# Two accumulator pools opened in the other order, in a hybrid DeltaNet/HGRN2 block

## The chip, the cores and the metric

One core of a Trainium2 chip runs the whole block. The metric is device time in microseconds, one launch, lower is better. Each kernel is run several times, and the median is compared.

## The reference, cut to what matters

The input x is 256 tokens by 2048 channels, float32. One layer is computed:

- `n = rms_norm(h)`, then one projection of `n` gives the inputs of 16 heads, 8 of gated DeltaNet ("GDN") and 8 of HGRN2, each 128 wide.
- each head runs its own chunked recurrence, is normalised per head and multiplied by a SiLU gate.
- `h = h + concat(y_A, y_B) @ W_out`, with `W_out` 2048 by 2048. Rows 0 to 1023 of it meet the GDN heads, rows 1024 to 2047 the HGRN2 heads.
- `h = h + relu(rms_norm(h) @ W1)^2 @ W2`, hidden width 8192, and a last `rms_norm`.

## The kernel before, in words

Each large product is done with a rounded part and its remainder: for a weight tile, `split` (L114) lets ScalarE write the rounded part `hi` (L120) and VectorE the difference `lo` (L121), and TensorE adds the products into one accumulator. Three stages follow one another.

**Input projection and heads.** The loop over `n` at L738 issues the projection of head `n + 1` and then the recurrence ("mix") of head `n`. The projections accumulate in pool `psP`, tiles `acc` (`acc_p("acc")`, L331 and L332) and `tok` (L358); the latter hold the values and gates of two heads, and ScalarE copies them out at L367. The mixes accumulate in pool `psM`: small products under the tag `mx` and those of the DeltaNet solve under `sv`. Each of the two pools holds four accumulators of 128x512 float32.

An HGRN2 mix (`hgrn_mix`, L633 to L732) is one dependent chain over several engines. Gates on ScalarE and VectorE (L641 to L656), one product on GpSimd (L657), a scan on VectorE (L659), two GpSimd steps (L660, L669), decays on VectorE and an exponential on ScalarE (L665, L671, L680, L681), then TensorE: scores inside 32-wide blocks into `pd` (L695, L698) and the others into `pa` (L704 to L710). VectorE masks and sums `pd` (L713, L717), GpSimd spreads the sum into `A` (L720), ScalarE copies `pa` into `A` (L723 to L727), TensorE multiplies `A` with the values into `poh` (L729 to L731). `finish_heads` takes it on: squares and a root on ScalarE (L479 to L481), the gate on VectorE (L483), a transpose on TensorE into `pt` (L487), and `hi` and `lo` of the result into `yTa` or `yTb` (L491, L492). In the first two HGRN2 heads the steps at L657, L660, L669 and L720 (`eng`) run on VectorE instead of GpSimd; the diff leaves that as it is, and the last two heads, of which the prediction speaks, have them on GpSimd.

**Output projection** (loop at L833). For each half `nh` of the output columns, 16 steps `k`, one per head: the weight rows of head `k` are split once, and 12 matmuls of 512 columns (L847) go into four accumulators. Step `k` reads `yT(k)`, the output of head `k`, so only steps 14 and 15 read the last two HGRN2 heads, called head 6 and head 7 below. The pools of the first stage are closed before (`mctx.close()`), and two new ones of four accumulators each are opened in their place, `psA` (`acc`) and then `psB` (`accb`). Half 0 accumulates in `psA`, half 1 in `psB`.

**MLP.** Both products, in `psA` and `psB` in turn (L876 to L878).

A closed pool's place is handed to whatever is opened next, from the front: `psA` lies where the pool opened first lay, `psB` where the second one lay. A tile in a new place waits for the last use of what lay there. A scheduler then puts the instructions of each engine in an order, and each engine works its list off in that order: an instruction that waits holds up all behind it. Weight tiles of 1 MB stream in on SyncE's queue (L304, L838, L951) through three buffers, `hi` and `lo` through three each, so that the split for step `k + 3` needs the matmuls of step `k` to be done.

The few lines that fix the places are these:

```
psM = mctx.enter_context(tc.tile_pool(name="psM", bufs=MXB, space=PSUM))
psP = mctx.enter_context(tc.tile_pool(name="psP", bufs=2, space=PSUM))
...
psA = ctx.enter_context(tc.tile_pool(name="psA", bufs=4, space=PSUM))
psB = ctx.enter_context(tc.tile_pool(name="psB", bufs=4, space=PSUM))
```

Of the kernel before, what the change touches and what calls it, by code (L numbers as in the profile page):

```python
# [12 lines left out]
PSUM = bass.MemoryType.PSUM  # L13
# [62 lines left out]
def hybrid_block(ctx: ExitStack, tc: tile.TileContext, x, xt, w_in, w_ab, params, w_out, w_ff1, w_ff2,  # L76
# [19 lines left out]
    yTa = ypool.tile([P, NYA, 2 * T], F32R, tag="yT", name="yTa")  # L96
    mctx = ExitStack()
    mp = mctx.enter_context(tc.tile_pool(name="mp", bufs=1))
    psM = mctx.enter_context(tc.tile_pool(name="psM", bufs=MXB, space=PSUM))
    psP = mctx.enter_context(tc.tile_pool(name="psP", bufs=2, space=PSUM))  # L100

    def wtile():
        return wpool.tile([P, 2048], F32, tag="w", name="w")
# [1081 lines left out]
```

## Time and profile before

| | |
|---|---|
| median of 3 runs | 1251.95 us (1251.02 to 1252.16) |
| the profiled execution: its own time | 1252.03 us |
| the profiled execution: span of the trace | 1250.2 us |
| mean granted TensorE clock | 0.98 of full speed |
| busy share: TensorE, VectorE, ScalarE, GpSimd | 98%, 83%, 62%, 9% |
| chain that ended last, share on TensorE | 91% |

The span runs from the first to the last instruction; 1.8 us of the execution lie around it. PE is TensorE, DVE VectorE, ACT ScalarE, POOL GpSimd. A row of the timeline has the start, the duration, the engine, the line, and what is written and read; in brackets stand the idle time before it and what ended that. The ends of matmuls are modelled, so that matmul rows overlap; the distance from one start to the next is the measure of their rate. A 32-bit product of two unrounded operands appears as two rows per matmul.

### The profile page before, as it was taken

Reading aid. Unit: us, or ns where it says so; the run is one execution under the profiler, and the core shown is the slowest. Engines: PE = TensorE matmul, PEld = TensorE weight load, DVE = VectorE, ACT = ScalarE, POOL = GpSimd, SP = SyncE. Lnnn points to the kernel's source line nnn. Section 1 sums busy time; section 2 is a strip of 40 time slices with the busy share of each in tenths; the row PEclk is TensorE's granted clock in tenths of the full one; section 3 lists DMA queues with packets and bytes.
Section 4 is the critical chain, followed back from the end, with each engine's and each line's share of the span. In section 5 each row is a group of like instructions: output and inputs, shape, how many; then the busy total and the mean of one; then the engine's idle time right before and its main releaser. Section 6 shows DMA issues by size and latency. Waiting matters only on the chain.

```text
span 1250.2 us, 18173 instructions
## 1 busy us (share of the span) xinstructions
PE 1221.6 (98%) x6894; PEld 1017.3 (81%) x6894; DVE 1035.3 (83%) x1455; ACT 777.0 (62%) x1150; POOL 113.4 (9%) x165
## 2 busy tenths in 40 slices
PE   9999999999999959999999999999999999999997
PEld 7888888887788848888888888888888888888886
DVE  7878997797778953768888889898998888988887
ACT  7668666675668653646655655666566656656553
POOL 0132333053111110000000000000000000000000
PEclk9999999999799969999999999999999999999999
DMA  9445555543235414665465455555775555565561
GB/s 332 167 161 193 169 184 175 204 168 120 76 129 203 169 69 163 241 198 201 169 230 204 169 203 209 173 185 181 262 281 198 196 208 202 176 228 196 177 233 68
DMA packets 37144, 233.45 MB, mean 187 GB/s; under 512 B 4696, under 2 KB 5728, under 8 KB 10176
## 3 DMA queue, kind: packets, MB, share of 16 engines
q1 hardware_dynamic: 34848, 229.83, 52.4%
q0 software_dynamic: 1632, 1.72, 0.6%
q8 instruction: 54, 0.88, 0.3%
q10 hardware_dynamic: 576, 0.74, 0.2%
q14 instruction: 34, 0.28, 0.1%
HBM read 227.67 MB, written 4.60 MB: 186 GB/s over the span
## 4 chain that ended last, share of the span: by engine, by line
PE 91%; POOL 2%; DVE 2%; DMA 2%; issue 1%; ACT 1%; SPq 0%; POOLq 0%; DVEq 0%; ACTq 0%
PE acc L877 9%; PE acc L878 9%; PE acc L876 9%; PE acc L358 9%; PE accb L877 8%; PE accb L876 8%; PE accb L878 8%; PE acc L331 8%; PE acc L332 4%; PE acc L847 4%; PE accb L847 3%; PE accv L331 2%; PE accv L332 1%; POOL X L513 1%; POOL Xt L511 1%
## 5 line engine op out<-in xcount | busy, mean ns | idle before, releaser
L121 DVE TENSOR_TENSOR lo<-w,hi 128x1024 fp32r<-128x1024 f32 (+1 forms) x422 | 485.7, 1167 | 123.4 <-ACT hi L120 112.3
L120 ACT CAST hi<-w 128x1024 fp32r<-128x1024 f32 (+1 forms) x422 | 413.7, 994 | 242.5 <-PE acc L877 56.2
L331 PE MATMUL acc<-xT,hi 128*128 128x512 f32 x512 | 181.2, 400 | 0.7 <-ACT hi L120 0.7
L332 PE MATMUL acc<-xT,lo 128*128 128x256 f32 x512 | 140.9, 287 | 0.0
L120 ACT CAST hi<-TT 128x1024 fp32r<-128x1024 f32 x88 | 92.0, 1052 | 77.5 <-issue 21.7
L121 DVE TENSOR_TENSOR lo<-TT,hi 128x1024 fp32r<-128x1024 f32 x88 | 106.8, 1221 | 30.4 <-ACT hi L120 28.1
L358 PE MATMUL acc<-hi,xT 128*128 128x512 f32 x384 | 117.6, 395 | 0.0
L331 PEld LDWEIGHTS acc<-xT,hi 128*128 128x128 f32 x512 | 95.4, 190 | 20.7 <-ACT hi L120 1.2
L332 PEld LDWEIGHTS acc<-xT,lo 128*128 128x128 f32 x512 | 97.2, 191 | 5.2 <-DVE lo L121 1.9
L876 PE MATMUL acc<-hi,sets 128*128 128x512 f32 x260 | 101.4, 391 | 0.0
L877 PE MATMUL acc<-hi,sets 128*128 128x512 f32 x260 | 101.2, 390 | 0.0
L878 PE MATMUL acc<-lo,sets 128*128 128x512 f32 x260 | 95.9, 390 | 0.0
L876 PE MATMUL accb<-hi,sets 128*128 128x512 f32 x224 | 88.0, 393 | 0.0
L877 PE MATMUL accb<-hi,sets 128*128 128x512 f32 x224 | 87.3, 390 | 0.0
L358 PEld LDWEIGHTS acc<-hi,xT 128*128 128x128 f32 x384 | 71.5, 189 | 14.9
L878 PE MATMUL accb<-lo,sets 128*128 128x512 f32 x224 | 78.7, 391 | 0.0
L877 PE MATMUL acc<-hi,gs 128*128 128x512 f32 (+1 forms) x200 | 77.0, 385 | 0.0
L876 PE MATMUL acc<-hi,gs 128*128 128x512 f32 (+1 forms) x200 | 76.7, 385 | 0.0
L878 PE MATMUL acc<-lo,gs 128*128 128x512 f32 (+1 forms) x200 | 75.6, 385 | 0.0
L358 PE MATMUL acc<-lo,xT 128*128 128x512 f32 x192 | 73.5, 401 | 0.0
L877 PE MATMUL accb<-hi,gs 128*128 128x512 f32 x188 | 73.1, 389 | 0.0
L876 PE MATMUL accb<-hi,gs 128*128 128x512 f32 x188 | 72.6, 389 | 0.0
(367 smaller groups left out, 2291.5 us busy)
## 6 DMA issues: line engine op xcount, KB each, us to landing
w<-in_w_ff_dram SPq DMA_DIRECT2D x128, 1024.0 KB, 5.0
w<-in_w_in_dram SPq DMA_DIRECT2D x61, 1024.0 KB, 5.0
w<-in_w_out_dram SPq DMA_DIRECT2D x16, 1024.0 KB, 5.0
w<-in_w_in_dram SPq DMA_DIRECT2D x12, 256.0 KB, 5.7
big<-in_xt_dram SPq DMA_DIRECT2D x8, 256.0 KB, 5.8
h<-in_x_dram SPq DMA_DIRECT2D x2, 1024.0 KB, 8.8
scr_h<-h SPq DMA_DIRECT2D x4, 512.0 KB, 7.7
tail<-scr_h SPq DMA_DIRECT2D x2, 1024.0 KB, 7.0
```

What stands on the lines that cost most here:

```text
L120: ACT.copy(hi, w)
L121: eng.tensor_tensor(out=lo, in0=w, in1=hi.bitcast(F32), op=ALU.subtract)
L331: PE.matmul(accs[g], lhsT=hi[:, kk, g, :], rhs=xT[:, k, :], start=(k == 0), stop=False)
L332: PE.matmul(accs[g][:, T:], lhsT=lo[:, kk, g, :], rhs=xT[:, k, 0:T], start=False, stop=(k == KT - 1))
L358: PE.matmul(accs[hf], lhsT=xT[:, k, a + hf * P:a + hf * P + P], rhs=ww[:, cs], start=(k == 0 and a == 0 and ww is hi), stop=(k == KT - 1 a ...
L511: POOL.tensor_tensor(out=t3, in0=X[:, j, j + 1:].unsqueeze(2).to_broadcast([P, nr, ncol]), in1=X[:, j, 0:ncol].unsqueeze(1).to_broadcast([ ...
L513: POOL.tensor_tensor(out=X[:, j + 1:, 0:ncol], in0=X[:, j + 1:, 0:ncol], in1=t3, op=ALU.subtract)
L847: PE.matmul(accs[2 * hf + c], lhsT=st, rhs=ww[:, c * 512:(c + 1) * 512], start=(k == 0 and a == 0 and ww is hi), stop=(k == 2 * NH - 1 and ...
L876: PE.matmul(dst, lhsT=ah, rhs=bh, start=start, stop=False)
L877: PE.matmul(dst, lhsT=al, rhs=bh, start=False, stop=False)
L878: PE.matmul(dst, lhsT=ah, rhs=bl, start=False, stop=stop)
```

## The change

The two pools of the first stage are opened in the other order. No size, no count and no line of the computation is touched.

```
     mctx = ExitStack()
     mp = mctx.enter_context(tc.tile_pool(name="mp", bufs=1))
+    psP = mctx.enter_context(tc.tile_pool(name="psP", bufs=2, space=PSUM))
     psM = mctx.enter_context(tc.tile_pool(name="psM", bufs=MXB, space=PSUM))
-    psP = mctx.enter_context(tc.tile_pool(name="psP", bufs=2, space=PSUM))
```

So `psA` now lies where the projections' accumulators were, and `psB` where those of the mixes were. The instructions are the same ones, and up to the scores of head 6 they stand in the same order on every engine. From there on the scheduler orders them otherwise, on TensorE, VectorE and ScalarE; the lists of GpSimd and SyncE stay as they were.

On TensorE, before: the rows from the transpose of head 6 to the first matmul of the output projection.

```order
L487 MATMUL pt<-cst,ig 128x128 x2
L695 MATMUL pd<-E 32x32 x32
L698 MATMUL pd<-gx 32x64 x8
L704 MATMUL pa<-E 32x32 x4
L708 MATMUL pa<-E 64x64 x2
L710 MATMUL pa<-L 128x128
L729 MATMUL poh<-ig,A 128x128
L730 MATMUL poh<-ig,A 128x128
L731 MATMUL poh<-ig,A 128x128
L487 MATMUL pt<-cst,ig 128x128 x2
L847 MATMUL acc<-hi,yTa 128x512 x4
```

All of head 7's products stand ahead of L847 there. On TensorE, now, the end of head 6's scores:

```order
L704 MATMUL pa<-E 32x32 x4
L708 MATMUL pa<-E 64x64 x2
L710 MATMUL pa<-L 128x128
L847 MATMUL acc<-hi,yTa 128x512 x4
L847 MATMUL acc<-lo,yTa 128x512 x2
```

The output projection now follows head 6's scores directly. What is left of the two heads stands between its matmuls: `poh` of head 6 in step 3, its `pt` and head 7's `pd` in step 6, head 7's `pa` in step 8, its `poh` in step 10 and its `pt` in step 12. Step 6 shows it, on TensorE, now:

```order
L847 MATMUL acc<-hi,yTa 128x512 x8
L847 MATMUL acc<-lo,yTa 128x512 x2
L487 MATMUL pt<-cst,ig 128x128 x2
L695 MATMUL pd<-E 32x32 x32
L698 MATMUL pd<-gx 32x64 x8
L847 MATMUL acc<-lo,yTa 128x512 x2
```

A transpose that waits there holds up the matmuls of the output projection behind it. On VectorE, in head 7's chain (`uz` and the second `ig` are the gate's, `lo<-w,hi` are splits of output weights), with - for before and + for now:

```order
 L375 SCALAR_TENSOR_TENSOR uz<-ig,uz 128x512
+L121 TENSOR_TENSOR lo<-w,hi 128x1024
 L659 SCALAR_TENSOR_TENSOR gx<-cst_a,u 128x256
 L377 TENSOR_TENSOR ig<-ig,uz 128x2x256
+L121 TENSOR_TENSOR lo<-w,hi 128x1024
 L665 TENSOR_TENSOR E<-gx 128x256 x5
-L483 SCALAR_TENSOR_TENSOR ig<-poh,ss,ig 128x128 x2
+L121 TENSOR_TENSOR lo<-w,hi 128x1024
 L682 TENSOR_TENSOR gx<-gx,u 128x256
 L680 TENSOR_TENSOR E<-E,gx 128x256 x5
 L681 TENSOR_TENSOR E<-E,gx 128x512
```

The splits of steps 3, 4 and 5, which stood behind the whole chain, now stand between its links, and head 6's gate (L483) has moved back past them. ScalarE's `hi` halves of the same splits moved in the same way.

More of the change, by code (lines that the diff above doesn't have):

```diff
@@ L98, in hybrid_block @@
     mp = mctx.enter_context(tc.tile_pool(name="mp", bufs=1))
+    psP = mctx.enter_context(tc.tile_pool(name="psP", bufs=2, space=PSUM))
     psM = mctx.enter_context(tc.tile_pool(name="psM", bufs=MXB, space=PSUM))
-    psP = mctx.enter_context(tc.tile_pool(name="psP", bufs=2, space=PSUM))
     def wtile():
```

## The prediction

> **What bounds the kernel now.** I read the page first: busy shares, then the forty slices.
>
> ```profile
> span 1250.2 us, 18173 instructions
> PE 1221.6 (98%) x6894; PEld 1017.3 (81%) x6894; DVE 1035.3 (83%) x1455; ACT 777.0 (62%) x1150; POOL 113.4 (9%) x165
> ...
> PE   9999999999999959999999999999999999999997
> ...
> PEclk9999999999799969999999999999999999999999
> ```
>
> TensorE is busy 98% of the span, so it sets the time. Only one slice falls clearly out, the fifteenth (437.6 to 468.8 us): PE is at 5 tenths there, and its granted clock at 6. That is where the input projection ends and the output projection begins. The view by windows cuts this place finer. Its columns are the window, its length, busy time (and count) of PE, PEld, DVE, ACT and POOL, the granted clock, the DMA share and GB/s.
>
> ```profile
> 440.00:450.00 10.00, 5.83 (x99) 4.28 (x97) 6.61 (x13) 8.11 (x16) 1.93 (x3) 0.93 0.53 201
> 450.00:460.00 10.00, 5.17 (x101) 4.16 (x101) 8.21 (x20) 4.47 (x13) 2.21 (x3) 0.50 0.00 1
> 460.00:470.00 10.00, 5.77 (x17) 4.34 (x18) 1.33 (x4) 2.54 (x11) 0.76 (x2) 0.50 0.01 2
> ...
> 513.35:1250.20 736.85, 728.67 (x3305) 604.79 (x3303) 632.76 (x782) 444.24 (x561) 1.13 (x2) 1.00 0.56 199
> ```
>
> From 450 to 470 the clock is half, and the DMA queues are all but silent. After 513 PE is busy 728.67 of 736.85 us at full clock, and the list of waits names none of PE's in that stretch: whatever is won before 513 should reach the end. PE's timeline shows who holds PE in the gap.
>
> ```profile
> 445.35 0.49 PE L710 MATMUL pa<-L 128*128 128x128 f32 x2
> 450.25 0.76 PE L729 MATMUL poh<-ig,A 128*128 128x128 f32 x2 [4.42 <-POOL u L657]
> ...
> 454.87 0.66 PE L487 MATMUL pt<-cst,ig 128*128 128x128 f32 x2 [3.01 <-DVE ig L483]
> 456.98 1.35 PE L695 MATMUL pd<-E 128*32 128x32 f32 x64 [1.45 <-DVE E L680]
> ...
> 461.87 0.77 PE L729 MATMUL poh<-ig,A 128*128 128x128 f32 x2 [1.20 <-POOL A L720]
> ...
> 465.44 0.66 PE L487 MATMUL pt<-cst,ig 128*128 128x128 f32 x2 [1.95 <-DVE ig L483]
> 467.19 2.08 PE L847 MATMUL acc<-hi,yTa 128*128 128x512 f32 x4 [1.08 <-DVE yTb L492]
> ...
> 472.47 1.14 PE L847 MATMUL acc<-hi,yTa 128*128 128x512 f32 x4
> ...
> 475.27 1.07 PE L847 MATMUL acc<-hi,yTa 128*128 128x512 f32 x4
> ...
> 477.99 1.07 PE L847 MATMUL acc<-hi,yTa 128*128 128x512 f32 x4
> ...
> 513.35 1.98 PE L847 MATMUL accb<-hi,yTa 128*128 128x512 f32 x8
> ```
>
> Between 445.84 (445.35 + 0.49) and 467.19 PE only follows the chain of heads 6 and 7, and the first L847 starts when the chain's last link, L492, is done. Step 0 of the output projection reads head 0 of the DeltaNet group, not head 7. What it waits for is the place of its accumulator: psA lies on psM, whose last user is head 7's transpose.
>
> **The change part by part.** No instruction is added or removed. The first L847 now needs the projections' accumulators, and their last reader is a copy on ScalarE:
>
> ```profile
> 445.04 0.69 ACT L367 ACTIVATE ig<-acc,gnw 128x512 f32<-128x512 f32 x1
> ...
> 447.10 0.63 ACT L217 ACTIVATE uz<-uz 128x512 f32<-128x512 f32 x1
> ...
> 471.86 1.05 ACT L120 CAST hi<-w 128x1024 fp32r<-128x1024 f32 x1 [5.25 <-PE acc L847]
> ```
> ```profile
> 445.17 1.23 DVE L121 TENSOR_TENSOR lo<-w,hi 128x1024 fp32r<-128x1024 f32 x1 [1.44 <-ACT hi L120]
> ```
>
> It ends at 445.73, before PE is through with head 6's scores. The splits of steps 0 to 2 exist by then: the third `lo` ends at 446.40, and the fourth `hi` waits for PE to let go of the first (5.25 us of idle, ended by L847). So the output projection can start at 445.9.
>
> *Its length.* A step at full clock is 477.99 − 475.27 = 2.72 us. The first step of before took 472.47 − 467.19 = 5.28 us at half clock and the second 2.80, 2.64 us too much in all. That is lost only because PE had idled; with no gap before it, it goes. Sixteen steps are 43.52 us.
>
> *What lies between them now.* The small products of the two heads were done inside the gap at half clock, and now take room among the L847. Their price at full clock is in rows of the same lines earlier in the trace:
>
> ```profile
> 428.37 0.38 PE L729 MATMUL poh<-ig,A 128*128 128x128 f32 x2
> ...
> 428.96 0.37 PE L332 MATMUL acc<-xT,lo 128*128 128x256 f32 x1
> ...
> 438.34 0.38 PE L487 MATMUL pt<-cst,ig 128*128 128x128 f32 x2
> 438.65 0.32 PE L695 MATMUL pd<-E 128*32 128x32 f32 x12
> ...
> 441.86 0.26 PE L695 MATMUL pd<-E 128*32 128x32 f32 x6
> 442.05 0.73 PE L358 MATMUL acc<-lo,xT 128*128 128x512 f32 x2
> ...
> 443.77 0.39 PE L358 MATMUL acc<-lo,xT 128*128 128x512 f32 x1
> 444.09 0.58 PE L695 MATMUL pd<-E 128*32 128x32 f32 x44
> ```
>
> A `poh` holds the stream up for 428.96 − 428.37 = 0.59 us, a `pt` for 438.65 − 438.34 = 0.31, and all scores of a head for 0.32 + 0.26 + (445.84 − 444.09) = 2.33. Two, two and one of them are left: 1.18 + 0.62 + 2.33 = 4.13 us. They can cost no less than nothing (half 0 would end at 489.4, the time be 1228.1) and hardly more than the 8.12 us that PE was busy with them in the gap at half clock (the row by windows under the rivals; 1236.2). I take 4.13, since it comes from the same products among full-rate matmuls.
>
> *Sum.* Half 0 ends at 445.9 + 43.52 + 4.13 = 493.55, where before it ended at 513.35: 19.8 us earlier. The profiled execution's 1252.03 becomes 1232.2; the median shown lies 0.08 below that execution, less than matters here.
>
> [...]
>
> *What hides the chain now.* Steps 14 and 15 need heads 6 and 7, and PE's fixed order puts the small products at set places, so each leg of the chain has the room between two places. Before, from the rows above, against the room now (2.72 a step, the small products added):
>
> - end of head 6's `pa` to its `poh`: 450.25 − 445.84 = 4.4 us before; room to the third matmul of step 3: 454.5 − 445.84 = 8.7.
> - `poh` to `pt` of head 6: 4.6 before; room to step 6: 465.1 − 454.5 = 10.6.
> - `pd` to `poh` of head 7: 4.9 before; room to step 10: 476.7 − 465.4 = 11.3.
> - `poh` to `pt` of head 7: 3.6 before; room to step 12: 6.7.
> - `pt` to the first reader of head 7: 1.75 before; room to step 15: 7.4.
>
> Into these legs go splits. One costs ScalarE 1.05 and VectorE 1.23 us, and it may also wait for PE to release a buffer, with the chain queued behind it. The first leg: `hi` of step 3 waits for the end of step 0 at 448.6, so the exponential behind it (L656) starts near 449.7 instead of 448.36, and the rest is late by 1.3 and one `lo`, 1.23: 4.4 becomes some 7, against 8.7. The second has three splits, of steps 4 to 6, one per 2.72 us. Counted on with the same durations, head 6's gate ends near 461.8 and is wanted at 465.1. The third and fourth leave about 3 us each. So the tightest slack is some 2 to 3 us.
>
> ```profile
> 424.00 1.22 DVE L121 TENSOR_TENSOR lo<-w,hi 128x1024 fp32r<-128x1024 f32 x1 [0.84 <-ACT hi L120]
> ```
> ```profile
> 424.58 1.25 POOL L657 TENSOR_TENSOR u<-u 128x256 f32<-128x256 f32 x1 [0.80 <-ACT u L656]
> ...
> 449.51 0.72 POOL L657 TENSOR_TENSOR u<-u 128x256 f32<-128x256 f32 x1
> ```
> ```profile
> 448.36 0.63 ACT L656 ACTIVATE u<-u 128x512 f32<-128x512 f32 x1 [0.63 <-DVE u L655]
> ```
> ```profile
> w<-in_w_out_dram SPq DMA_DIRECT2D x16, 1024.0 KB, 5.0
> ```
>
> GpSimd's step takes 1.25 us beside a split on VectorE and 0.72 without one; now splits run beside all of head 7's GpSimd steps. At 0.53 us for each of five that is 2.7 us over three legs, at most 1 to 1.6 in one. Weights hold: a tile lands in 5.0 us and feeds two steps, 5.44. Half 1 needs psB, now on psM, and head 7's transpose is read some 8 us before 493.55.
>
> **The rivals.** *The chain comes late.* A slack of 2 to 3 us is small for work queued behind splits, and a late link stops PE itself, since the product that wants it stands in front of L847 rows. For it: each GpSimd row of head 7 may stretch, and VectorE has 12.6 us of chain work in this stretch. Against it: the legs' sums above. If one leg runs 3 us over its slack, the time is 1235; if two do and each stop also costs the clock, at 2.64 us, it is 1232.2 + 6 + 5.3 = 1243.5. [...]
>
> ```profile
> 445.84:467.19 21.35, 8.12 (x111) 6.26 (x111) 12.62 (x31) 9.91 (x31) 4.89 (x7) 0.57 0.09 37
> ```
>
> *Slower, by lockstep.* Were every one of the old waits paid again inside the output projection (21.35 − 8.12 = 13.2 us of idle) and the stops kept the clock at half, as from 450 to 470, all sixteen steps would cost 5.28 instead of 2.72, 41 us more. The gain of 19.8 is gone once, beside 13.2 us of stops, three more steps run cold (3 × 2.56 = 7.7). With six cold steps it is 1232.2 + 13.2 + 15.4 = 1260.8. Against it: the old waits were exposed because nothing else was queued, and now 2.72 us of ready work stands ahead of each.
>
> *No change.* The pools swap, but the wait moves to half 1, whose place is now psM: it would have to wait until 513. For that, head 7 would have to end 20 us later than the 485 worked out here. Or the placement is not what I read it to be, and the first L847 still waits for head 7; but its order, ahead of head 7's products, would then stop the program.
>
> **How the numbers follow.** The full gain, 1230.5 to 1235, has 0.80; the late chain, 1235 to 1244, 0.14; lockstep 0.03; no change 0.03. The range goes from 1230, where the small products hide better than priced, to 1241, which takes in most of the second case. Faster by over 0.2% (2.5 us, about what a measurement here can tell from no change) is 0.80 + 0.14 = 0.94, same 0.03, slower 0.03.
>
> **What would show it.** In the changed profile the fifteenth slice should read 9 for PE and for the clock, half 0 should start at 445.9 and its L847 rows come every 2.72 us from the first; `accb` should start near 493.5, and DMA should move some 190 GB/s from 450 to 470. PE's waits should name neither L483, L720 nor L492. A wait at L487 or L729 among L847 rows would show the late chain, and its length the loss; a clock of 0.50 in such a window the lockstep. If `accb` starts at 493.5 and the end does not come 19.8 us earlier, my claim that PE sets all that follows is wrong.

## The result, and the profile after

The changed kernel takes 1232.41 us, the median of 4 runs (1231.15 to 1233.91), beside 1252.06 us for the kernel before in as many (1251.02 to 1253.11). The ratio is 0.9844, with a 95% interval of 0.9826 to 0.9861. The forecast was 1232.2.

The profiled execution is the slowest of the four, 1233.91 us. Its page, busy shares first and then the slices:

```profile
span 1232.1 us, 18170 instructions
PE 1217.8 (99%) x6894; PEld 1014.9 (82%) x6894; DVE 1035.6 (84%) x1455; ACT 776.3 (63%) x1150; POOL 113.9 (9%) x165
...
PE   9999999999999999999999999999999999999997
...
PEclk9999999998799999999999999999999999999999
```

The fifteenth slice, 5 and 6 before, reads 9 for PE and for the clock. The view by windows, columns as before, puts numbers to the same place:

```profile
440.00:450.00 10.00, 10.00 (x116) 7.75 (x117) 7.68 (x14) 8.63 (x15) 0.98 (x2) 1.00 0.61 211
450.00:460.00 10.00, 10.00 (x49) 8.38 (x48) 8.84 (x17) 7.46 (x17) 3.74 (x4) 1.00 0.39 120
460.00:470.00 10.00, 10.00 (x121) 8.17 (x121) 7.90 (x13) 4.27 (x7) 0.00 (x0) 1.00 0.52 198
493.50:1232.00 738.50, 730.23 (x3310) 605.52 (x3308) 634.02 (x784) 444.64 (x561) 1.12 (x2) 1.00 0.56 199
```

PE is busy in all of every window, at full clock, and the weights keep coming. From 450 to 470 DMA moves 120 and 198 GB/s, 159 on average, where 190 was expected. PE's timeline shows what fills the stretch:

```profile
446.29 0.49 PE L710 MATMUL pa<-L 128*128 128x128 f32 x2
446.72 1.21 PE L847 MATMUL acc<-hi,yTa 128*128 128x512 f32 x4
...
449.62 1.07 PE L847 MATMUL acc<-hi,yTa 128*128 128x512 f32 x4
...
452.34 1.07 PE L847 MATMUL acc<-hi,yTa 128*128 128x512 f32 x4
...
455.51 0.38 PE L729 MATMUL poh<-ig,A 128*128 128x128 f32 x2
...
456.10 0.71 PE L847 MATMUL acc<-hi,yTa 128*128 128x512 f32 x2
...
466.19 0.38 PE L487 MATMUL pt<-cst,ig 128*128 128x128 f32 x2
466.50 0.73 PE L695 MATMUL pd<-E 128*32 128x32 f32 x62
...
467.42 0.73 PE L847 MATMUL acc<-lo,yTa 128*128 128x512 f32 x2
...
477.72 0.38 PE L729 MATMUL poh<-ig,A 128*128 128x128 f32 x2
...
484.54 0.38 PE L487 MATMUL pt<-cst,ig 128*128 128x128 f32 x2
...
491.84 1.07 PE L847 MATMUL acc<-hi,yTb 128*128 128x512 f32 x4
...
494.56 1.98 PE L847 MATMUL accb<-hi,yTa 128*128 128x512 f32 x8
```

The first L847 stands right behind L710, and no row of PE from 446 to 495 has a bracket: it waits for nothing there. Half 0 lasts 494.56 − 446.72 = 47.84 us; 47.65 was forecast, and before it was 513.35 − 467.19 = 46.16, with almost nothing between its steps. `accb` starts 18.8 us earlier than before instead of 19.8. The missing us was lost ahead of the change's place: L710 ends at 446.78 here and at 445.84 in the execution of before, and the first L847 is late by the same 0.9 (the last section shows where it was lost). From `accb` to the end of the span it takes 737.54 us against 736.85. Both differences lie within the scatter of single executions; the runs of this kernel differ by 2.8 us.

From the end of L710 to the first `accb` it was 513.35 − 445.84 = 67.51 us before, and it is 494.56 − 446.78 = 47.78 now. By the rows, the 19.7 us between them are made up of 13.2 us of idle PE, 4 us of small products (8.12 at half clock, 4.1 to 4.3 now) and some 2.5 us of cold first steps, steps at half clock.

### The profile page after: what moved, and what is told of

Read it like the earlier page. It is cut to its first block, busy times and chain, and to the rows that moved or that the text cites. A ratio compares the mean times of both kernels' runs of the same rounds, so it can differ in the third digit from the quotient of the medians.

```text
span 1232.1 us, 18170 instructions
## 1 busy us (share of the span) xinstructions
PE 1217.8 (99%) x6894; PEld 1014.9 (82%) x6894; DVE 1035.6 (84%) x1455; ACT 776.3 (63%) x1150; POOL 113.9 (9%) x165
## 4 chain that ended last, share of the span: by engine, by line
PE 91%; DMA 2%; DVE 2%; POOL 2%; issue 2%; ACT 1%; SPq 0%; POOLq 0%; DVEq 0%; ACTq 0%
PE acc L877 9%; PE acc L876 9%; PE acc L878 9%; PE acc L358 9%; PE accb L878 8%; PE accb L877 8%; PE acc L331 8%; PE accb L876 8%; PE acc L332 4%; PE acc L847 4%; PE accb L847 4%; PE accv L331 2%; PE accv L332 1%; POOL X L513 1%; POOL Xt L511 1%
```

## The experiments

The theory was the prediction's: half 0 had waited for the place of its accumulators, not for data, and ready matmuls now fill the waits of the last heads' chain. The rivals were that the exchange does something else, that a late chain costs part of the gain, and that the clock rather than the waits made the loss. The runs were made in three groups, each beside runs of the kernel before on the same chip (medians 1252.26, 1252.78 and 1252.66); the ratios of this section are to those.

**The place alone, from both sides.** The kernel before, with the output stage's pools exchanged instead of the first stage's:

```
-    psA = ctx.enter_context(tc.tile_pool(name="psA", bufs=4, space=PSUM))
     psB = ctx.enter_context(tc.tile_pool(name="psB", bufs=4, space=PSUM))
+    psA = ctx.enter_context(tc.tile_pool(name="psA", bufs=4, space=PSUM))
```

> The kernel before, its two first-stage pools in the old order (psM, then psP), but with psB opened ahead of psA, so that half 0 of the output projection accumulates where the projections did. Theory (what counts is only on whose place half 0's accumulators lie): the instructions come in the order of the changed kernel, and the time is the changed kernel's, 1232.4 us, within 2; half 0 starts near 446 to 447 us and ends near 494. Rival (the order of the pools in the first stage, or the banks the mixes and projections themselves use, made the gain): the time stays at 1252.

Measured: 1232.56 us (1232.44 to 1234.39), ratio 0.9843 [0.9828, 0.9858]. All its engines have the changed kernel's order of instructions. The windows from 450 to 470 and the start of half 1:

```profile
450.00:460.00 10.00, 10.00 (x49) 8.38 (x48) 8.89 (x16) 7.19 (x15) 4.69 (x5) 1.00 0.32 105
460.00:470.00 10.00, 10.00 (x121) 8.18 (x121) 7.99 (x14) 5.18 (x9) 0.00 (x0) 1.00 0.62 213
```
```profile
495.48 1.98 PE L847 MATMUL accb<-hi,yTa 128*128 128x512 f32 x8
```

The same edit in the changed kernel puts `psA` back on the mixes' place:

> The changed kernel (psP, then psM) with psB opened ahead of psA, so that half 0 lies on the mixes' accumulators again. Theory: the gain is gone, 1252 us within 2, with the first L847 near 467 us, after head 7's last link, and half the clock from 450 to 470. Rival (the gain comes from the projections' and mixes' own banks in the first stage): 1232.

Measured: 1252.71 us (1250.90 to 1255.33), ratio 1.0002 [0.9993, 1.0012]. The first L847 waits for L492 as before:

```profile
467.73 2.08 PE L847 MATMUL acc<-hi,yTa 128*128 128x512 f32 x4 [1.08 <-DVE yTb L492]
```

What counts is the pairing, which pool of the second stage lies on which of the first, and nothing else in the change.

**The place without the data.** The changed kernel with half 0's steps in reverse, so that it begins with head 7, and with its start and stop flags moved along:

```
-        for kp in range(8):
+        for kp in range(7, -1, -1) if nh == 0 else range(8):
...
-            for kk in range(2):
+            for kk in (1, 0) if nh == 0 else (0, 1):
...
```

> The changed kernel with half 0's sixteen steps in reverse, head 7 first; the sums are the same in another order. The place is free as in the changed kernel, but now the data of the first step is head 7's. Theory (the gain is the time in which PE has steps to do that need nothing of heads 6 and 7; the free place only allows it): the wait comes back whole, first L847 near 467 us, 1252 us within 2. Rival (the place alone, or the scheduler's other order of splits, makes the gain): 1232 to 1240.

Measured: 1252.24 us (1248.28 to 1253.56), ratio 0.9997 [0.9988, 1.0006]. The place is free, but the first step's data are not:

```profile
467.24 2.93 PE L847 MATMUL acc<-hi,yTb 128*128 128x512 f32 x6 [0.56 <-ACT yTb L491]
```

So a free place is worth nothing by itself. The gain is the work that needs neither head 6 nor head 7 and can stand ahead of them.

**Half of the place.** In the kernel before, the accumulators under `sv` and those under `mx` become two pools, and `psA` two pools of two accumulators each, so that the first two of half 0 lie on places that come free early:

```
-    psM = mctx.enter_context(tc.tile_pool(name="psM", bufs=MXB, space=PSUM))
+    psV = mctx.enter_context(tc.tile_pool(name="psV", bufs=4 - MXB, space=PSUM)); psM = mctx.enter_context(tc.tile_pool(name="psM", bufs=MXB, space=PSUM))
...
-    psA = ctx.enter_context(tc.tile_pool(name="psA", bufs=4, space=PSUM))
+    psA = [ctx.enter_context(tc.tile_pool(name=f"psA{i}", bufs=2, space=PSUM)) for i in range(2)]; nA = [0]
...
```

> The kernel before with the pools of the solve (two accumulators), the mixes (two) and the projections (four) opened in this order and psA split into two pools of two: half 0's accumulators for the first 128 tokens lie on the solve's place, free since long, those for the other 128 on the mixes'. Theory: only the first-token matmuls of the steps whose splits exist can go ahead, three buffers of them, 3 x 6 x 0.227 = 4.1 us of work, into the first wait of 4.4 us. The other waits stay, and the clock falls later by about those 4.1 us: 1246 to 1248 us. Rival (any free accumulator lets the whole stage start): 1232 to 1236. Rival (one accumulator in the mixes' place holds all back): 1252.

Measured: 1247.15 us (1246.20 to 1248.76), ratio 0.9958 [0.9943, 0.9972]. PE's timeline:

```profile
445.10 1.17 PE L847 MATMUL acc<-hi,yTa 128*128 128x512 f32 x4
...
449.61 0.46 PE L729 MATMUL poh<-ig,A 128*128 128x128 f32 x2 [0.15 <-POOL u L657]
...
454.24 0.50 PE L487 MATMUL pt<-cst,ig 128*128 128x128 f32 x2 [3.73 <-DVE ig L483]
...
466.55 2.08 PE L847 MATMUL acc<-hi,yTa 128*128 128x512 f32 x4 [1.08 <-DVE yTb L492]
```

Three half steps (445.10 to about 449.2) fill the first wait, 4.42 us before and 0.15 now. Then the ready work is used up, and the rest is paid as before. The gain, some 5 us, is about the length of the work that was moved (3 × 1.36 = 4.08 us).

In the control the first-stage pools are divided in the same way, but `psA` stays one pool of four:

> The kernel before with the solve's two accumulators, the mixes' two and the projections' four opened as three pools in this order, and psA left as one pool of four: two of half 0's accumulators lie on the solve's place and two on the mixes'. The instructions come in the order of the kernel before. Theory (a pool's first tile waits for all that lay under the pool): 1252 us within 2. Rival (a tile waits only for what lay under it): as half_place, 1246 to 1248.

Measured: 1252.11 us (1250.66 to 1253.31), ratio 0.9996 [0.9986, 1.0005].

```profile
468.05 2.08 PE L847 MATMUL acc<-hi,yTa 128*128 128x512 f32 x4 [1.08 <-DVE yTb L492]
```

Two of the four places under `psA` were free at 445, as the run before shows, and the first accumulator waited until 468 for all of them. In this program a pool's first tile waits for everything that lay under the whole pool.

**The clock by itself.** The first try at keeping the clock up in the kernel before, without moving any work, was dummy products that nobody reads, behind head 6's scores and behind its `poh`:

```
+    def dummies(a, b, n):
+        if n:
+            t = sv("dummy")
+            for _ in range(n):
+                PE.matmul(t[:, 0:b.shape[-1]], lhsT=a, rhs=b, start=True, stop=True)
...
+        dummies(xT[:, 0, 0:P], xT[:, 0, :], 18 if hd == 6 else 0)
...
+        dummies(A[:, 0:P], A[:, 0:P], 10 if hd == 6 else 0)
```

> The kernel before with 18 products of 512 columns and 10 of 128 that nobody reads (into an accumulator of the solve), put on TensorE between head 6's scores and its poh and between that poh and its transpose, so that the clock should not fall; 14 and 10 of them stand in the two longest waits, 4 a little earlier where they cost up to 0.9 us. The waits for the chain stay. Theory (of the 19.8 us, 2.64 was the cold first steps, and 8.12 - 4.13 = 4.0 the small products at half clock, most of them links of the chain): granted clock 0.9 or more from 450 to 470, and 2.64 + 4.0 - 0.9, about 4 to 6 us gained: 1246 to 1248 us. Rival (the clock is a side show, the idle time is all): 1250 to 1253. Rival (the clock is most of it): below 1240.

Measured: 1253.62 us (1252.78 to 1255.90), ratio 1.0006 [0.9997, 1.0016]. A miss: in the profiled execution, the longest of the ten, the clock fell all the same, though no wait of PE was longer than 1.95 us. Its mean clock was 0.982, that of the others 0.983 to 0.985, and 0.980 to 0.982 without the dummies. Its windows, and PE's timeline (L847 is L855 there):

```profile
450.00:460.00 10.00, 5.75 (x110) 4.77 (x108) 7.17 (x19) 4.84 (x16) 3.41 (x5) 0.86 0.00 1
460.00:470.00 10.00, 5.67 (x26) 4.35 (x27) 2.50 (x7) 2.54 (x11) 0.76 (x2) 0.50 0.01 2
```
```profile
456.07 0.50 PE L487 MATMUL pt<-cst,ig 128*128 128x128 f32 x2 [1.49 <-DVE ig L483]
458.18 1.36 PE L701 MATMUL pd<-E 128*32 128x32 f32 x64 [1.62 <-DVE E L686]
...
468.38 2.08 PE L855 MATMUL acc<-hi,yTa 128*128 128x512 f32 x4 [1.08 <-DVE yTb L492]
```

The scores behind the second of these waits already run at half speed: 1.36 us for 64 rows of L701, where 62 of the same product took 0.73 in the changed kernel.

The second try put dummies into all six waits, each group on a tile that is written no earlier than its wait begins:

```
+        dummies(ivg[:, 1, 0:P], ivg[:, 1, 0:T], 8 if hd == 6 else 0)
+        dummies(E[:, 0, 0:P], E[:, 1, :], 2 if hd == 7 else 0)
...
+        dummies(A[:, 0:P], A[:, 0:P], {6: 14, 7: 7}.get(hd, 0))
...
+        dummies(yT(NH + hd, 0, P), xT[:, 0, :], {6: 3, 7: 2}.get(hd, 0))
```

> A second try at the clock alone: the kernel before with products that nobody reads in all six waits of the gap, each group reading a tile that is written no earlier than the wait begins, so that none runs ahead of it. The waits for the chain stay, and nothing of the output projection moves. Theory (of the 19.8 us, 13.2 were idle time, 4.0 the small products at half clock, 2.6 the cold first steps): granted clock 0.95 or more from 450 to 470, small products at their full-clock prices, step 0 of the output projection 2.72 to 2.9 us; 6.6 us gained, less up to 0.9 for two groups that come in the way of the scores: 1245.5 to 1248. Rival (the clock is a side show): 1251 to 1253. If the clock falls again, the question stays open.

Measured: 1250.89 us (1249.75 to 1254.14), ratio 0.9991 [0.9980, 1.0002], which tells it neither from no change nor, surely, from a small gain. The windows of the profiled execution, again the longest of the ten, and PE's timeline (L847 is L856):

```profile
450.00:460.00 10.00, 7.56 (x61) 5.91 (x60) 7.17 (x19) 4.85 (x16) 3.41 (x5) 0.90 0.00 1
460.00:470.00 10.00, 7.51 (x105) 6.26 (x104) 2.28 (x7) 2.54 (x11) 0.76 (x2) 0.76 0.01 2
```
```profile
459.33 2.08 PE L636 MATMUL dummy<-E 128*128 128x256 f32 x4
...
465.06 0.77 PE L736 MATMUL poh<-ig,A 128*128 128x128 f32 x2 [1.93 <-POOL A L727]
...
466.48 2.59 PE L636 MATMUL dummy<-A 128*128 128x128 f32 x14
...
470.64 1.19 PE L856 MATMUL acc<-hi,yTa 128*128 128x512 f32 x4
```

The granted clock was 0.90 and 0.76 where 0.95 or more was expected: it fell twice, though it came back each time. The first step is warm here, 473.51 − 470.64 = 2.87 us by the start of the next one, so a clock that is up does spare the cold step. But the first L847 comes 3.4 us later than the 467.19 of before. Of these, 1.2 us had been lost ahead of the gap (the scores of head 6 end at 447.04 instead of 445.84); the rest is that dummies stood in the chain's way, the group on `E` amid the scores and the group on `A`. In this execution the two about cancel. Six of the ten executions took 1249.75 to 1250.90 us at a mean clock of 0.989 or 0.990, about that of the changed kernel, and the other four 1252.66 to 1254.14 at 0.985 to 0.987; only the longest has a profile. What the clock alone is worth is therefore not measured by either run.

**How much lateness the cover takes.** In the changed kernel GpSimd multiplies head 7's gate by 1.0 a number of times ahead of its scan, which makes all of head 7's chain late and changes no value:

```
         eng.tensor_tensor(out=lf[:, 0, :], in0=lf[:, 0, :], in1=lf[:, 1, :], op=ALU.add)
+        for _ in range(8 if hd == 7 else 0): POOL.tensor_scalar(lf[:, 0, :], lf[:, 0, :], 1.0, None, ALU.mult)
```

With 8, 16 and 28 passes:

> The changed kernel with eight further GpSimd passes over head 7's 128x256 log decays (times 1.0, so that nothing changes in value), 7 to 9 us more in the chain ahead of its scan. The scheduler knows of them and puts head 7's products later. Theory: the chain ended at 486 us and step 15 begins at 491.8, and the chain without its waits for PE's places is some 17 to 20 us from the scan (452.3) on, so about 20 us of delay are free: 1232.4 us within 2. Rival of the prediction, the late chain (slack of 2 to 3 us a leg is all there is): 4 to 6 us lost, 1236 to 1239.

> The changed kernel with 16 further GpSimd passes in head 7's chain; at the 1.23 to 1.27 us that one took in the kernels with 8 and 28, some 20 us more. Theory (about 20 us are covered by the sixteen steps): at the edge, 1232 to 1235 us. Rival (the cover is that of the single legs, 4 us each): 1240 or more, since 28 passes cost 14.8 us and 12 fewer would then save less than 8.

> The same with 28 further passes, 24 to 32 us more in head 7's chain. [...] If the cover is larger than worked out, 1232.

| passes | they took | time, us | ratio [interval] | PE's waits in half 0 |
|---|---|---|---|---|
| 0 (the change) | 0 | 1232.41 | 0.9844 [0.9826, 0.9861] | none |
| 8 | 9.81 us | 1231.95 (1231.73 to 1233.91) | 0.9834 [0.9819, 0.9848] | none |
| 16 | 20.04 us | 1236.59 (1235.33 to 1238.28) | 0.9874 [0.9852, 0.9895] | 1.90, 0.56 |
| 28 | 35.51 us | 1247.23 (1246.06 to 1247.73) | 0.9951 [0.9936, 0.9966] | 6.33, 1.51, 1.90, 0.56 |

The rows that carry the table: with 8 passes, on GpSimd, then with 16, on PE, and with 28, on PE (L847 is L848 in all three).

```profile
451.18 9.81 POOL L658 TENSOR_SCALAR u<-u 128x256 f32<-128x256 f32 x8
```
```profile
491.34 0.49 PE L487 MATMUL pt<-cst,ig 128*128 128x128 f32 x2 [1.90 <-DVE ig L483]
492.40 2.93 PE L848 MATMUL acc<-hi,yTb 128*128 128x512 f32 x6 [0.56 <-ACT yTb L491]
496.63 1.08 PE L848 MATMUL accb<-hi,yTa 128*128 128x512 f32 x4
```
```profile
495.12 0.44 PE L696 MATMUL pd<-E 128*32 128x32 f32 x16 [6.33 <-DVE E L681]
```

A chain that is 9.8 us late costs nothing: the scheduler puts head 7's products at later places among the L847, and the slack of the single legs does not matter. At 20.0 us the ready work runs out just before the end. The loss of some 4 us there is 1.90 + 0.56 us of waits and a last step that runs partly cold (496.63 − 492.40 = 4.23 instead of 2.72). At 35.5 us the loss is 14.8: 10.3 us of waits (6.33 + 1.51 + 1.90 + 0.56), and the rest is cold products between and behind them. The run with 16 passes came out 1.6 us above the 1235 that its expectation ended at, and the one with 28 passes 1.2 us above the 1236 to 1246 put down for it; that one's passes also took 35.5 us, longer than the 24 to 32 expected of them. Half 0 thus covers a delay of more than 9.8 and less than 20.0 us. An estimate of the point between does not hold: less its 2.5 us of waits the row with 16 passes would put it near 17.5, but the row with 28, less its 10.3, near 25.2.

## Why the prediction was right, point by point

The mechanism, the range and the path came out as forecast. That the median came within 0.2 us of 1232.2 is closer than the runs of one kernel agree (2.8 us), and in part luck, as the terms below show.

- *The wait for the place* was the cause. It is shown by the exchange from either side (0.9843 and 1.0002), and the half place shows that it can be had in parts.
- *Ready data* were the condition: with the place free and head 7 first, the gain is nil (0.9997).
- *Steps of 2.72 us.* The steps with nothing between them took 2.72 to 2.74, save the first, 449.62 − 446.72 = 2.90. The L847 of half 0 come at their full rate from its second step on.
- *Small products, 4.13 us.* The five steps with small products among them took 3.41, 4.08, 3.80, 3.42 and 2.99 us, together 4.10 more than 2.72 each. With 0.18 in the first step and 0.04 in three others, that is all of the 4.3 us (47.84 − 43.52) that the sixteen steps took over 43.52. The sum was right, its terms less so. A `poh` stands in 456.10 − 455.51 = 0.59 as priced, but the two L847 behind it take 0.1 us longer than elsewhere, so its step is 0.69 or 0.70 longer. The first `pt` and the scores made their two steps 1.36 and 1.08 longer, 2.44 where 0.31 + 2.33 was put. The 0.2 too little and the 0.2 too much cancel.
- *The change from full-width to 32-wide products and back*, in steps 6 and 8, left no cost of its own to see on top of the 4.13. But that price was itself read from 32-wide products among full-width ones, so what the change alone costs the rows do not tell. The two L847 behind the 32-wide products of step 6 took 467.99 − 467.42 = 0.57 us, against 0.46 elsewhere; behind a full-width `poh`, with no 32-wide product near, two took 456.65 − 456.10 = 0.55. From the end of L710 to `accb` the time shrank by 19.7 us, where the sum of the prediction had 19.8.
- *Slack of the legs.* It was better than the "2 to 3 us" written. The products that PE took without waiting were ready well ahead, as VectorE's rows show for the two gates and for the last link:

```profile
462.06 0.60 DVE L483 SCALAR_TENSOR_TENSOR ig<-poh,ss,ig 128x128 f32<-128x128 f32 x2
...
479.95 0.61 DVE L483 SCALAR_TENSOR_TENSOR ig<-poh,ss,ig 128x128 f32<-128x128 f32 x2 [0.58 <-ACT ss L481]
...
485.47 0.48 DVE L492 SCALAR_TENSOR_TENSOR yTb<-pt,gnw,yTb 128x256 fp32r<-128x256 f32 x1
```

Head 6's gate is done at 462.66 and its transpose is taken at 466.19, 3.5 us later. The forecast was 461.8 and 465.1, 3.3 apart; they came 0.9 and 1.1 later, with the 0.9 that the whole stage was late. Head 7's `poh` has 4.1 us (ScalarE's last copy into `A` ends at 473.62, and it is taken at 477.72), its gate 4.0 (480.56 to 484.54), the last link 5.9 (485.95 to 491.84). The tightest slack was thus 3.5 us.

- *The first leg was misread*, on the safe side. The prediction took it to lengthen from 4.4 to "some 7 against 8.7", since the list of waits puts head 6's `poh` down to L657. But `poh` reads `A` and `ig`, not `u`. What it truly waited for is ScalarE's copy into `A`, which ended at nearly the same time. PE's weight load for `poh` (PEld) tells the two apart in the kernel before:

```profile
450.22 0.50 PEld L729 LDWEIGHTS poh<-ig,A 128*128 128x128 f32 x2 [4.58 <-POOL u L657]
```

It starts at 450.22, just before L657 ends (449.51 + 0.72 = 450.23), and so it does in the two runs with divided pools (449.57 against 449.59, 451.08 against 451.09). The copy, first in the kernel before, then in the changed one, on ScalarE:

```profile
449.74 0.41 ACT L727 COPY A<-pa 32x64 f32<-32x64 f32 x2
```
```profile
450.99 0.41 ACT L727 COPY A<-pa 32x64 f32<-32x64 f32 x2
```

It ends at 450.15 there, and `poh` starts at 450.25; now it ends at 451.40 and `poh` is taken at 455.51. From the end of L710 the leg is 4.3 us before and 4.6 now. The copy stands behind the exponential (L656), which came 1.0 us later after L710, but it does not stand behind L657, and before it had waited 0.58 us for GpSimd's L720 anyway. So only 0.3 us of the lateness reached it, and the slack is 4.1 us where 8.7 − 7 = 1.7 was written.

- *GpSimd beside VectorE.* L657 stretched to 1.25 us, as priced; L669 took 1.02 instead of 0.85, and L660 its 1.13 as before. First GpSimd's rows, then VectorE's splits beside them:

```profile
451.02 1.25 POOL L657 TENSOR_TENSOR u<-u 128x256 f32<-128x256 f32 x1 [0.68 <-ACT u L656]
453.16 1.13 POOL L660 TENSOR_SCALAR gx<-gx 128x256 f32<-128x256 f32 x1 [0.89 <-DVE gx L659]
```
```profile
450.45 1.23 DVE L121 TENSOR_TENSOR lo<-w,hi 128x1024 fp32r<-128x1024 f32 x1 [0.37 <-ACT hi L120]
...
453.50 1.42 DVE L121 TENSOR_TENSOR lo<-w,hi 128x1024 fp32r<-128x1024 f32 x1
```

L657 begins 0.57 us into its split and ends 0.59 us after it. Beside L660 it was the split that took longer, 1.42 us against 1.23. Head 7's L720 (0.76 us, from 470.09) had no split beside it. These rows show that L657 is slower beside a split, 1.25 us against 0.72 without one; by what, they do not show. It costs no time here.

- *The cold steps and half-clock products*, some 6.5 us of the gain, are accounting from rows. Neither try at keeping the kernel before warm isolated them, so this share is argued, not shown. That a warm first step is 2.87 instead of 5.28 us is shown.
- *Lockstep* did not occur with stops of 1.90 and 0.56 us in the run with 16 passes: only the step behind them was slow.

## What to carry to other kernels

Where a stage's first matmuls wait for the last link of the stage before, look whether they read what it wrote or only stand where it stood: if the ready half can lie on memory that comes free early, a serial chain, of 21 us here, can disappear among full-rate matmuls. What makes it work is ready work queued ahead of the late products, and its cover has an end: half 0 of 47 us took a further 9.8 us of lateness for nothing and lost 4 us at 20. A wait's named releaser is the one that came last, and where the waiting instruction does not read what it wrote, another row of about the same end has to be looked for before the leg is counted on. Here the waiting one had even begun 0.01 us before the named one ended.

## What the runs showed of the hardware that was not expected

The clock falls to half without one long pause. With the first dummies PE waited 1.49 and 1.62 us, with 0.5 us of transpose between them, and the scores behind ran at half speed; with 16 late passes 1.90 and 0.56 us around one transpose were enough to make the next six matmuls take 2.93 us. With the second dummies a single wait of 1.93 us was enough: read in windows of 0.1 us, the granted clock fell at 464.9, 1.8 us after PE's last product (463.14). In the kernel before it fell 2.9 us after the last product (448.7 against 445.84), and in the half place 4.2 us after L731, with one transpose in between (454.7 against 450.5). So no one length of wait decides in these profiles.

A busy PE is not always at full clock either. Far from the change, TensorE works on small products of the solve and on rows of the projection between them. First the changed kernel, then a longer window of the kernel before:

```profile
330.00:340.00 10.00, 10.00 (x63) 8.76 (x63) 4.67 (x9) 3.08 (x10) 2.87 (x5) 0.50 0.00 1
```
```profile
324.00:339.40 15.40, 15.40 (x113) 13.24 (x114) 9.86 (x21) 4.19 (x12) 3.32 (x5) 0.50 0.17 65
```

In the kernel before PE has no wait from 323.95 on, and the full clock came back only at 339.5, 15.5 us later, while behind the gap 5.4 us of L847 had been enough (467.19 to 472.6). What makes the difference no run here shows. In the changed kernel it came back at 341.4, and that is where the 0.9 us were lost: the two profiled executions are 0.07 us apart at L597 (339.48 and 339.55) and 0.95 at L729 (342.02 and 342.97). Where this stretch ends differs from one execution to the next, whichever the order of the pools: with that of before L729 comes at 342.02, 342.79 (the first dummies) and 343.95 (`psB` ahead of `psA`), with that of the change at 342.97, 341.78 (8 passes) and 341.04 (16 passes).
